# A transformer-like layer on one core: all chains of the activation sums ahead of the 1/rms scaling, in the openings of both SwiGLUs

## The chip, the core and the metric

The kernel runs on one core of a Trainium2 chip. The core has TensorE (PE: matmuls), VectorE (DVE) and ScalarE (ACT) for element by element work, GpSimd (POOL) and SyncE (SP), which issues the DMAs here. Each engine works through its own queue in order; semaphores make one wait for another. The metric is the device time of one execution in microseconds, the median of several runs.

## The reference

The layer has 1024 tokens of width 1024, in float32. What the change touches are the two SwiGLU sub-layers, the first and the last of four:

```python
def rmsnorm(x, g):
    y = xf * lax.rsqrt(jnp.mean(xf * xf, axis=-1, keepdims=True) + EPS)
    return (y * g.astype(jnp.float32)).astype(x.dtype)

def swiglu(h, w_gu, w_down):
    gate, up = jnp.split(h @ w_gu, 2, axis=-1)
    return (jax.nn.silu(gate) * up) @ w_down

x = x + 0.5 * swiglu(rmsnorm(x, ffn1_norm), ffn1_w_gu, ffn1_w_down)
...
x = x + 0.5 * swiglu(rmsnorm(x, ffn2_norm), ffn2_w_gu, ffn2_w_down)
```

The hidden width is 2816. Between the two stand two token mixers and a cross attention; they and the final norm are the same in both kernels.

## The kernel before, in words

Activations are held with the width on the 128 partitions and the tokens along the row: `x{c}_{hf}` is chunk `c` (0 to 7) of the width and half `hf` (0, 1) of the tokens, 128 x 512. A float32 product is made of three matmuls in the format fp32r: every operand is split into a high part (ACT copies it) and a low part (DVE subtracts), and high x high, high x low and low x high are added up in a PSUM bank. The gain is applied to x beforehand; the factor 1/rms belongs to a token and is multiplied in after the matmul (`rs`, a tile for each half of the tokens).

The SwiGLU's products go through a Strassen-Winograd scheme on 2 x 2 blocks: seven products instead of eight (`PRODUCTS`, line 235), from sums of the weights (`S1` to `S4`, made on POOL) and sums of the activations (`T1` to `T4`). The products of a job accumulate in three bank names X, Y, Z with two banks each. For a job the order is A11 into X, S1 x T1 into Y, S2 x T2 into X, A12 into Z, S3 x T3 into X, S4 into Y, A22 x T4 into X. After A11, S1 and S2 ACT copies the bank to SBUF (`e<-X`, `e<-Y`, `E<-X`); the next product into the bank waits for that copy.

The sums of the activations are made for four quarters `j` (two chunks of the width each) by `sums_12` (line 657), a generator that is one chain: POOL forms the difference `S<-x,x`; ACT makes the high part of T1 and a scaled copy `e` or `t`; DVE makes the low part of T1 and then T2 in `e` or `t`; ACT makes T2's high part and DVE its low part. A slot for `S` is one of three, so the fourth difference needs the first chain's slot back, when ACT and DVE have read it. `flow` (line 641) writes several chains in turns, a step of each. `sums_4` and `sums_3` make T4 and T3 later.

The opening of a SwiGLU, up to `pairs.run()` (line 968), runs ahead of the scheme. The first two columns of gate and up are computed plainly, eight chunks each (`plain`, and the gates before it): in the first SwiGLU the gates lie in PSUM banks X and Y, in the second (`stored`) they were computed earlier, written to DRAM and loaded again, half of them into a slot for weights (`r`). `scaled` (line 909) multiplies a gate column by `rs` on DVE and applies SiLU on ACT; the first SiLU needs a table load. `between` (line 929) is a generator that scales the four gate columns and then has `pairs.start` write the first loads, sums and splits of the scheme's weights. It is written as a third chain among `sums_12`, with a width of three chains.

In the first SwiGLU 1/rms comes from eight squares of token rows on ACT (line 470); the tiles of the last four are loaded once the first four are done with. A root of twelve small DVE steps follows, then PE spreads it over the partitions (line 218) and ACT copies it to `rs`. In the second SwiGLU the root is done before the opening.

The order of each engine is set by the written order: `in_order` (line 70) makes every instruction issued through `dve`, `act`, `pl_` and `pe` follow the one issued before on that engine, and all the steps above go through it. Instructions outside it (the squares, the root, the first factors) are fitted in between by the framework's scheduler when the kernel is built. In the profile most of these lines show as the helper's line 82.

Of the kernel before, what the change touches and what calls it, by code (L numbers as in the profile page):

```python
# [8 lines left out]
F32 = mybir.dt.float32  # L9
# [9 lines left out]
P = 128  # L19
# [3 lines left out]
H = 512  # L23
# [8 lines left out]
def hybrid_layer(ctx, tc, x, x_cols, mem, gains, ffn1_w_gu, ffn1_w_down, w_in, w_out, mem_w_q, mem_w_kv, mem_w_o,  # L32
# [6 lines left out]
    def pool(stack, name, bufs=1, space=None, side=None):  # L39
        kw = {} if space is None else {"space": space}  # L40
        if side:
            kw["side"] = side
        return stack.enter_context(tc.tile_pool(name=name, bufs=bufs, reuse_waits="tile", **kw))
# [386 lines left out]
    with ExitStack() as st:  # L430
# [48 lines left out]
        for e in range(2):  # L479
            own, other = (slice(64 * i, 64 * i + 64) for i in (e, 1 - e))  # L480
            t = maskp.tile([P, P], F32R, name=f"swap{e}")
# [4 lines left out]
        for n in (1, 2):  # L486
# [22 lines left out]
            for i in range(2):  # L509
                t = maskp.tile([P, P], F32R, name=f"yy{n}_{i}")  # L510
# [92 lines left out]
    def slot(blk, key, j):  # L603

        if key in ("T1", "T2", "T4"):
            t = blk.sum_slot(key, j)
            return t[:, 0, :], t[:, 1, :]
        c, hf = {"B11": (2 * j, 0), "B21": (2 * j + 1, 0), "B22": (2 * j + 1, 1), "T3": (2 * j, 1)}[key]
        return hp.tile([P, H], F32R, name=f"hh{c}_{hf}"), hp.tile([P, H], F32R, name=f"hl{c}_{hf}")
# [4 lines left out]
    def swiglu(rs, ys, g0, w_gu, w_down, blk, first, tag, done, tail, head, stored=False, hook=None, side=None, plain_last=False, lift=None):  # L614
        with ExitStack() as st:
# [19 lines left out]
            def quarter(j):  # L635
                return ([xT[2 * j + k, hf] for k in range(2) for hf in range(2)]
                        + [G[:, g0 + 2 * j + k:g0 + 2 * j + k + 1] for k in range(2)])
# [3 lines left out]
            def flow(chains, width):  # L641

                chains, active = list(chains), []
                while chains or active:
                    while chains and len(active) < width:
                        active.append(chains.pop(0))
                    active = [c for c in active if next(c, active) is not active]

            def chain_part(key, src, j):
                hi, lo = slot(blk, key, j)  # L650
                act.activation(hi, src, AF.Copy)
                yield
                dve.tensor_tensor(lo, src, hi.bitcast(F32), op=ALU.subtract)
                B[key].append((hi, lo))
                yield

            def sums_12(j, t):
                x11, x12, x21, x22, g1, g2 = quarter(j)
                d = blk.sp.tile([P, 4, P], F32, name="S").rearrange("p a b -> p (a b)")
                ts[j] = t  # L660
                hi, lo = slot(blk, "T1", j)
                pl_.tensor_tensor(d, x12, x11, op=ALU.subtract)
                yield
                act.activation(hi, d, AF.Copy, scale=g1)
                act.activation(t, d, AF.Copy, scale=g1)
                yield
                dve.scalar_tensor_tensor(lo, d, g1, hi.bitcast(F32), op0=ALU.mult, op1=ALU.subtract)
                B["T1"].append((hi, lo))
                dve.scalar_tensor_tensor(t, x22, g2, t, op0=ALU.mult, op1=ALU.subtract)
                yield  # L670
                yield from chain_part("T2", t, j)
# [10 lines left out]
            def sums_4(j):  # L682
                x11, x12, x21, x22, g1, g2 = quarter(j)
                dve.scalar_tensor_tensor(ts[j], x21, g2, ts[j], op0=ALU.mult, op1=ALU.subtract)
                yield
                yield from chain_part("T4", ts[j], j)
# [220 lines left out]
            pairs = weave(*streams)  # L907

            def scaled(out, src, hf):
                to = src if stored else out  # L910
                dve.tensor_tensor(to, src, rs[hf], op=ALU.mult)
                yield
                act.activation(out, to, AF.Silu)
                yield
# [13 lines left out]
            tp = pool(tps, "tp", 2)  # L928
            def between():
                for hf, src in ((0, early), (1, late)):  # L930
                    for m in range(2):
                        yield from scaled(s[hf][m], src[m], hf)
                pairs.start(1)
                yield
                pairs.start(2)
                yield
                pairs.start(3)

            flow([sums_12(j, pools["e0"].tile([P, H], F32, name="e") if j < 2 else tp.tile([P, H], F32, name="t"))
                  for j in range(2)] + [between()]  # L940
                 + [sums_12(j, tp.tile([P, H], F32, name="t")) for j in range(2, 4)], 3)
            flow([sums_4(0), sums_4(1)], 2)
            for m in range(2):
                dve.tensor_tensor(s[0][m], s[0][m], ups[0][m], op=ALU.mult)
# [47 lines left out]
    def to_mixers(acc, psn, psg, sgp):  # L992
        for c in range(DC):
# [4 lines left out]

    xs = {}
    swiglu(rs1, [y1[:, 0:4], y1[:, 4:8]], GF1, ffn1_w_gu, ffn1_w_down, blk1, first, "f", lambda d, hf, sqp, acc: arrive(d, hf, GMIX, sqp, acc, False, (d, hf) in ((7, 0), (6, 1))),  # L1000
           to_mixers, gps, hook=lower_bound, side=normalise_memory, lift=GMIX)
    f1.close()
# [664 lines left out]
    with ExitStack() as f2:  # L1667
        blk2 = blocks(f2, True)
        first = [blk2.load(ffn2_w_gu, 0, 4, FF)]
        swiglu(rs, ys2, GF2, ffn2_w_gu, ffn2_w_down, blk2, first, "g", arrive_last, finish, gd, True, plain_last=True)  # L1670
# [30 lines left out]
```

## Time and profile before

| | |
|---|---|
| median of 3 runs | 2307.11 us (2306.14 to 2309.64) |
| the profiled execution's time | 2306.37 us |
| its span, first to last instruction | 2304.7 us |
| PE busy | 2222.0 us, 96% |
| DVE, ACT, POOL busy | 73%, 43%, 32% |
| PE's mean granted clock | 0.988 |
| first opening in the trace | from 7 us to 72 us |
| second opening | from 1646 us to 1687 us |

Sums are made against the profiled execution, whose time is 0.74 us below the median. Matmuls overlap a little, so a row's duration is not the step from one to the next.

### The profile page before, as it was taken

How to read it: one execution, taken by the hardware profiler on the slowest of the kernel's cores; microseconds unless marked ns; L12 is line 12 of the kernel's file. 1: busy time of each engine (PE TensorE's matmuls, PEld its weight loads, DVE VectorE, ACT ScalarE, POOL GpSimd, SP SyncE). 2: the span in 40 equal slices, each digit the busy share in tenths (PEclk: the TensorE clock that was granted, in tenths of full speed). 3: DMA queues.
4: the chain of work that ended last, by engine and by line, in shares of the span. 5: the costliest groups of instructions: out<-in, count | busy, mean ns of one | idle time of the engine just before them, and what ended most of it. 6: DMA issues, size and time to landing. Idle time of an engine off the chain costs nothing. (4 is left out here: it accounts for less than half of the span.)

```text
span 2304.7 us, 31240 instructions
## 1 busy us (share of the span) xinstructions
PE 2222.0 (96%) x11240; PEld 1863.5 (81%) x11240; DVE 1681.3 (73%) x2816; ACT 984.1 (43%) x1877; POOL 732.8 (32%) x685
## 2 busy tenths in 40 slices
PE   8899999999999999999989999999989999999997
PEld 7788888778778797888879888887778888878876
DVE  6877778868976869778697546567587676885796
ACT  6544444443345526344364333224454343444324
POOL 3353536534541102010031020001335353653553
PEclk9999999999989999999999999999999999999999
DMA  8344443666721000100115311111334333366652
GB/s 293 115 137 136 139 136 134 241 217 216 238 94 38 28 20 28 32 24 28 38 30 163 110 37 56 46 37 42 124 110 138 112 135 119 128 239 215 194 174 74
DMA packets 220571, 265.80 MB, mean 115 GB/s; under 512 B 13440, under 2 KB 144512, under 8 KB 220416
## 3 DMA queue, kind: packets, MB, share of 16 engines
q1 hardware_dynamic: 220416, 263.80, 34.6%
q8 instruction: 89, 1.46, 0.3%
q14 instruction: 66, 0.54, 0.1%
HBM read 187.47 MB, written 76.28 MB: 114 GB/s over the span
## 5 line engine op out<-in xcount | busy, mean ns | idle before, releaser
L82 PE MATMUL X<-T,f 128*128 128x512 f32 x1464 | 348.4, 394 | 12.9 <-ACT e L82 12.6
L82 PEld LDWEIGHTS X<-T,f 128*128 128x128 f32 x1464 | 277.6, 190 | 72.5 <-ACT e L82 13.5
L82 PE MATMUL X<-hh,f 128*128 128x512 f32 x975 | 315.1, 394 | 8.8 <-DVE E L82 7.8
L82 ACT ACTIVATE f<-S 128x512 fp32r<-128x512 f32 (+2 forms) x256 | 155.3, 608 | 266.0 <-POOL S L82 252.3
L82 DVE TENSOR_TENSOR f<-S,f 128x512 fp32r<-128x512 f32 (+2 forms) x256 | 233.7, 925 | 38.8 <-ACT f L82 38.2
L82 PEld LDWEIGHTS X<-hh,f 128*128 128x128 f32 x975 | 184.6, 189 | 51.1 <-issue 9.2
L82 POOL TENSOR_TENSOR E<-E,rs 128x512 f32<-128x512 f32 x112 | 183.3, 1637 | 123.1 <-DVE E L82 102.7
L82 DVE TENSOR_TENSOR f<-r,f 128x512 fp32r<-128x512 f32 (+2 forms) x192 | 202.4, 1071 | 0.1
L82 PE MATMUL X<-hl,f 128*128 128x512 f32 x488 | 192.1, 394 | 2.9 <-DVE hl L82 2.9
L82 POOL TENSOR_TENSOR S<-r,r 128x512 f32<-128x512 f32 (+2 forms) x64 | 94.0, 1469 | 304.0 <-DMA r<-in_ffn_w_down_dram 84.8
L82 PE MATMUL Y<-T,f 128*128 128x512 f32 x732 | 176.4, 390 | 0.0
L82 PE MATMUL Z<-hh,f 128*128 128x512 f32 x488 | 161.0, 390 | 0.0
L82 PE MATMUL Y<-hh,f 128*128 128x512 f32 x488 | 160.9, 390 | 0.0
L82 PEld LDWEIGHTS Y<-T,f 128*128 128x128 f32 x732 | 137.5, 188 | 28.5
L127 PE MATMUL acc<-hh,wh 128*128 128x512 f32 (+1 forms) x384 | 153.7, 400 | 3.5 <-DVE E L82 3.2
L128 PE MATMUL acc<-hl,wh 128*128 128x512 f32 (+1 forms) x384 | 145.9, 380 | 1.9 <-DMA hl<-msl 1.9
L82 POOL TENSOR_TENSOR S<-S,r 128x512 f32<-128x512 f32 (+2 forms) x64 | 83.5, 1304 | 197.5 <-DVE f L82 173.3
L129 PE MATMUL acc<-hh,wl 128*128 128x512 f32 (+1 forms) x384 | 145.9, 380 | 0.0
L1123 POOL TENSOR_SCALAR_AFFINE_SELECT om<-om 128x128 f32<-128x128 f32 x64 | 26.8, 418 | 357.4 <-ACT om L1118 357.2
L82 DVE TENSOR_TENSOR E<-X,E 128x512 f32<-128x512 f32 x98 | 67.3, 687 | 93.1 <-PE X L82 92.4
L82 ACT ACTIVATE E<-X 128x512 f32<-128x512 f32 x102 | 60.4, 592 | 170.8 <-PE X L82 170.8
L107 ACT ACTIVATE wh<-wraw 128x512 fp32r<-128x512 f32 (+1 forms) x128 | 79.0, 654 | 106.4 <-PE acc L128 39.8
(453 smaller groups left out, 5476.5 us busy)
## 6 DMA issues: line engine op xcount, KB each, us to landing
r<-in_ffn_w_gu_dram SPq DMA_DIRECT2D x86, 512.0 KB, 3.6
r<-in_ffn_w_down_dram SPq DMA_DIRECT2D x32, 512.0 KB, 4.1
wraw<-in_w_in_dram SPq DMA_DIRECT2D x20, 512.0 KB, 3.6
wraw<-in_mem_w_kv_dram SPq DMA_DIRECT2D x16, 512.0 KB, 3.8
x<-in_x_cols_dram SPq DMA_DIRECT2D x16, 256.0 KB, 5.4
T<-in_x_dram SPq DMA_DIRECT2D x8, 512.0 KB, 6.4
fx<-x SPq DMA_DIRECT2D x16, 256.0 KB, 5.1
sg<-fx SPq DMA_DIRECT2D x16, 256.0 KB, 4.2
```

What stands on the lines that cost most here:

```text
L82: done = getattr(self.eng, name)(*args, **kw)
L107: nc.scalar.activation(hi[:, part], src[:, part], AF.Copy)
L127: nc.tensor.matmul(ps, lh, rh, start=start, stop=False)
L128: nc.tensor.matmul(ps, lh, rl, start=False, stop=False)
L129: last_mm[0] = nc.tensor.matmul(ps, ll, rh, start=False, stop=stop).ins
L1123: nc.gpsimd.affine_select(out=a[:, dg], in_=a[:, dg], compare_op=ALU.is_gt, fill=fill, base=0, pattern=[[-1, P]], channel_multiplier=1)
```

## The change

The four chains of `sums_12` are written in one `flow` of width three. `between`, which scales the gate columns, is written behind them. The first loads, sums and splits of the scheme (`pairs.start`) move into a function `factors_first`: in the first SwiGLU it is called at the end of `between` as before, in the second ahead of it. No instruction is added or removed, and no tile changes its size.

```diff
                 for hf, src in ((0, early), (1, late)):
                     for m in range(2):
                         yield from scaled(s[hf][m], src[m], hf)
-                pairs.start(1)
-                yield
-                pairs.start(2)
-                yield
-                pairs.start(3)
+                if not stored:
+                    factors_first()
+
+            def factors_first():
+                for n in (1, 2, 3):
+                    pairs.start(n)
 
             flow([sums_12(j, pools["e0"].tile([P, H], F32, name="e") if j < 2 else tp.tile([P, H], F32, name="t"))
-                  for j in range(2)] + [between()]
-                 + [sums_12(j, tp.tile([P, H], F32, name="t")) for j in range(2, 4)], 3)
+                  for j in range(4)], 3)
+            if stored:
+                factors_first()
+            for _ in between():
+                pass
             flow([sums_4(0), sums_4(1)], 2)
```

How it moves the instructions is shown at three places. Names carry the tile's number behind the underscore: `T12` is the sum T1 of quarter 2, `T20` the sum T2 of quarter 0.

ACT in the first opening, from the first factor of the up columns (line 422) on; the rows of line 470 are the squares. Before:

```order
L422 ACTIVATE f_542<-r0_141 128x512 [waits DMAHW3_49]
L422 ACTIVATE f_545<-r1_143 128x512 [waits DMAHW4_49]
L422 ACTIVATE f_548<-r0_141 128x512
L470 ACTIVATE T43_322,ss8_321<-T43_322 128x1024 [waits DMAHW5_49]
L470 ACTIVATE T40_325,ss8_321<-T40_325 128x1024 [waits DMAHW6_49]
L470 ACTIVATE T41_328,ss8_321<-T41_328 128x1024 [waits DMAHW7_49]
L470 ACTIVATE T42_331,ss8_321<-T42_331 128x1024 [waits DMAHW0_49]
L422 ACTIVATE f_551<-r1_143 128x512 [waits DVE_49,PE_49]
L470 ACTIVATE T43_334,ss8_321<-T43_334 128x1024 [waits DMAHW1_49,Activation_49]
```

And now:

```order
L422 ACTIVATE f_542<-r0_141 128x512 [waits DMAHW3_49]
L82 ACTIVATE T12_642<-S_641,G_83 128x512 [waits Pool_49]
L82 ACTIVATE t_633<-S_641,G_83 128x512
L422 ACTIVATE f_545<-r1_143 128x512 [waits DMAHW4_49]
L422 ACTIVATE f_548<-r0_141 128x512
L82 ACTIVATE T20_656<-e_631 128x512 [waits DVE_49]
L470 ACTIVATE T43_322,ss8_321<-T43_322 128x1024 [waits DMAHW5_49]
L82 ACTIVATE T21_658<-e_632 128x512 [waits DVE_49]
L470 ACTIVATE T40_325,ss8_321<-T40_325 128x1024 [waits DMAHW6_49]
L82 ACTIVATE T22_660<-t_633 128x512 [waits DVE_49]
L470 ACTIVATE T41_328,ss8_321<-T41_328 128x1024 [waits DMAHW7_49]
L82 ACTIVATE T13_666<-S_665,G_83 128x512 [waits Pool_49]
```

Six of the chains' copies stand between the factors and among the squares now (two more follow, behind the fifth and the sixth square), and five of these six rows wait for DVE or POOL.

DVE in the first opening. Before, behind the root (its last step is the row just ahead of these):

```order
L79 TENSOR_TENSOR sg_624<-X_145,rs0_584 128x512 [waits Activation_49]
L82 SCALAR_TENSOR_TENSOR T10_636<-S_635,G_83,T10_636 128x512 [waits Pool_49]
L82 SCALAR_TENSOR_TENSOR e_631<-x1_1_127,G_83,e_631 128x512
L82 SCALAR_TENSOR_TENSOR T11_639<-S_638,G_83,T11_639 128x512 [waits Pool_49]
L82 SCALAR_TENSOR_TENSOR e_632<-x3_1_131,G_83,e_632 128x512
L82 TENSOR_TENSOR sg_625<-Y_156,rs0_584 128x512
L82 TENSOR_TENSOR T20_652<-e_631,T20_652 128x512 [waits Activation_49]
L82 TENSOR_TENSOR T21_654<-e_632,T21_654 128x512 [waits Activation_49]
L82 TENSOR_TENSOR sg_626<-X_239,rs1_591 128x512 [waits PE_49]
```

Now, ahead of the root; the rows of line 191 and 423 are splits that stood there before as well:

```order
L82 SCALAR_TENSOR_TENSOR e_631<-x1_1_127,G_83,e_631 128x512
L191 SCALAR_TENSOR_TENSOR hl7_1_312<-x7_1_139,G_83,hh7_1_311 128x512 [waits DMAHW2_49,Activation_49]
L82 SCALAR_TENSOR_TENSOR T11_639<-S_638,G_83,T11_639 128x512 [waits Pool_49]
L423 TENSOR_TENSOR f_542<-r0_141,f_542 128x512 [waits DMAHW3_49,Activation_49]
L82 SCALAR_TENSOR_TENSOR e_632<-x3_1_131,G_83,e_632 128x512
L423 TENSOR_TENSOR f_545<-r1_143,f_545 128x512 [waits DMAHW4_49,Activation_49]
L423 TENSOR_TENSOR f_548<-r0_141,f_548 128x512 [waits Activation_49]
L82 SCALAR_TENSOR_TENSOR T12_642<-S_641,G_83,T12_642 128x512 [waits Pool_49]
L82 SCALAR_TENSOR_TENSOR t_633<-x5_1_135,G_83,t_633 128x512
L82 TENSOR_TENSOR T20_656<-e_631,T20_656 128x512 [waits Activation_49]
L82 TENSOR_TENSOR T21_658<-e_632,T21_658 128x512 [waits Activation_49]
L82 TENSOR_TENSOR T22_660<-t_633,T22_660 128x512 [waits Activation_49]
```

The chains stood behind the scaling `sg_624<-X_145,rs0_584`, which waits for ACT's copy of 1/rms; they stand ahead of the root now, and the scaling is the first row behind it.

DVE in the second opening, behind the low parts of the up factors. Before:

```order
L82 TENSOR_TENSOR sg_15882<-sg_15882,rs0_15842 128x512 [waits DMAHW2_49,Activation_49,Pool_49]
L82 SCALAR_TENSOR_TENSOR T10_15899<-S_15898,G_83,T10_15899 128x512 [waits Pool_49]
L82 SCALAR_TENSOR_TENSOR e_15894<-x1_1_11857,G_83,e_15894 128x512
L82 SCALAR_TENSOR_TENSOR T11_15902<-S_15901,G_83,T11_15902 128x512 [waits Pool_49]
L82 SCALAR_TENSOR_TENSOR e_15895<-x3_1_12803,G_83,e_15895 128x512
L82 TENSOR_TENSOR sg_15883<-sg_15883,rs0_15842 128x512 [waits DMAHW3_49]
L82 TENSOR_TENSOR T20_15915<-e_15894,T20_15915 128x512 [waits PE_49,Activation_49]
L82 TENSOR_TENSOR T21_15917<-e_15895,T21_15917 128x512 [waits PE_49,Activation_49]
L82 TENSOR_TENSOR r0_15886<-r0_15886,rs1_15849 128x512 [waits DMAHW7_49]
L82 TENSOR_TENSOR r0_15886<-r0_15886,rs1_15849 128x512 [waits DMAHW4_49]
```

And now:

```order
L82 SCALAR_TENSOR_TENSOR T10_15899<-S_15898,G_83,T10_15899 128x512 [waits Activation_49]
L82 SCALAR_TENSOR_TENSOR e_15894<-x1_1_11857,G_83,e_15894 128x512 [waits Activation_49]
L82 SCALAR_TENSOR_TENSOR T11_15902<-S_15901,G_83,T11_15902 128x512 [waits Activation_49]
L82 SCALAR_TENSOR_TENSOR e_15895<-x3_1_12803,G_83,e_15895 128x512 [waits Activation_49]
L82 SCALAR_TENSOR_TENSOR T12_15905<-S_15904,G_83,T12_15905 128x512 [waits PE_49,Activation_49]
L82 SCALAR_TENSOR_TENSOR t_15896<-x5_1_11845,G_83,t_15896 128x512 [waits Activation_49]
L82 TENSOR_TENSOR T20_15919<-e_15894,T20_15919 128x512 [waits PE_49,Activation_49]
L82 TENSOR_TENSOR T21_15921<-e_15895,T21_15921 128x512 [waits PE_49,Activation_49]
L82 TENSOR_TENSOR T22_15923<-t_15896,T22_15923 128x512 [waits Activation_49]
L82 SCALAR_TENSOR_TENSOR T13_15929<-S_15928,G_83,T13_15929 128x512 [waits Activation_49]
L82 SCALAR_TENSOR_TENSOR t_15897<-x7_1_12747,G_83,t_15897 128x512 [waits Activation_49]
L82 TENSOR_TENSOR T23_15935<-t_15897,T23_15935 128x512 [waits Activation_49]
```

The scaling was first and the low parts of T12 and T13 came behind the first factor of the scheme; now all chains are done first, three low parts of the scheme's factors (`f`) follow, and the scaling is next.

## The prediction

> **What bounds the kernel now.** I began with the page's busy line and its group of TensorE's costliest waits, then the list of who waited for whom.
>
> ```profile
> PE 2222.0 (96%) x11240; PEld 1863.5 (81%) x11240; DVE 1681.3 (73%) x2816; ACT 984.1 (43%) x1877; POOL 732.8 (32%) x685
> PE X L82 <- ACT e L82: 12.6, 2, 6.7
> ```
>
> TensorE (PE) is busy 96% of the span, so an edit can earn only where PE stands still. The second row is PE's largest sum of waits: two waits on ScalarE's (ACT's) copy `e`, 12.6 us in all, one in each SwiGLU. The timeline of PE shows both.
>
> ```profile
> 57.20 2.88 PE L82 MATMUL Y<-T,f 128*128 128x512 f32 x12
> 66.75 5.49 PE L82 MATMUL X<-T,f 128*128 128x512 f32 x12 [6.67 <-ACT e L82]
> 72.03 0.53 PE L82 MATMUL Z<-hh,f 128*128 128x512 f32 x1
> ...
> 1673.49 2.88 PE L82 MATMUL Y<-T,f 128*128 128x512 f32 x12
> 1682.35 5.08 PE L82 MATMUL X<-T,f 128*128 128x512 f32 x12 [5.98 <-ACT e L82]
> 1687.28 0.40 PE L82 MATMUL Z<-hh,f 128*128 128x512 f32 x1
> ```
>
> In each opening the second sum product (T2 into bank X) starts 6.0 to 6.7 us late (a row: start, duration, engine, line, operation, tiles; in brackets the idle time before it and what ended it), and then takes 5.1 to 5.5 us, where the twelve matmuls of T1 just before took 2.88. The table by stretches gives the reason (columns: stretch; its length; busy time and count of PE, weight load, VectorE (DVE), ACT, POOL; granted clock; DMA share; GB/s):
>
> ```profile
> 62.00:72.20 10.20, 5.46 (x13) 4.30 (x14) 9.67 (x17) 6.23 (x12) 0.00 (x0) 0.50 0.13 51
> 1679.90:1686.70 6.80, 4.35 (x10) 3.49 (x11) 6.77 (x12) 3.70 (x8) 0.00 (x0) 0.51 0.21 80
> ```
>
> After the idle stretch the granted clock is half. So a stall is paid twice. From the end of T1 to the first Z matmul the first opening takes 72.03 − 60.08 = 11.95 us, the second 1687.28 − 1676.37 = 10.91; twelve matmuls at full clock advance the queue by 2.72 (the quoted 2.88 less the overlap of the last one). **Recoverable: 9.2 us and 8.2 us.**
>
> Why is ACT late? Its queue and DVE's, first opening:
>
> ```profile
> 62.84 1.29 ACT L82 ACTIVATE T<-e 128x512 fp32r<-128x512 f32 x2 [3.75 <-DVE e L82]
> 66.12 0.57 ACT L82 ACTIVATE e<-X 128x512 f32<-128x512 f32 x1
> 39.81 0.69 DVE L79 TENSOR_TENSOR sg<-X,rs 128x512 f32<-128x512 f32 x1 [2.68 <-ACT rs L221]
> 59.73 2.35 DVE L82 TENSOR_TENSOR T<-t,T 128x512 fp32r<-128x512 f32 x2
> 41.29 1.68 POOL L82 TENSOR_TENSOR S<-x,x 128x512 f32<-128x512 f32 x1 [22.72 <-DMA fx<-x]
> 1654.80 0.69 DVE L82 TENSOR_TENSOR sg<-sg,rs 128x512 f32<-128x512 f32 x1 [5.35 <-ACT rs L221]
> 1656.29 1.68 POOL L82 TENSOR_TENSOR S<-x,x 128x512 f32<-128x512 f32 x1 [14.04 <-DVE T L82]
> 1656.73 1.79 DVE L82 SCALAR_TENSOR_TENSOR T<-S,G,T 128x512 fp32r<-128x512 f32 x1
> ```
>
> `e<-X` stands behind T4's first parts on ACT, these behind DVE's `e`, that behind the low parts of T2 (59.73). And all DVE work of the chains stands behind one instruction, the scaling `sg<-X,rs`, which needs 1/rms. While it waits, POOL idles 22.72 and 14.04 us, because the fourth difference needs a slot that DVE must first free (the first row names the DMA; the order of instructions has POOL wait for DVE). The last row shows a DVE step that takes 1.79 us while POOL works.
>
> **The change, second opening.** The 16 chain steps of DVE now stand ahead of the scaling, and ACT's chain steps stand around the two copies of rs. 1/rms itself isn't touched: its root stands ahead of all this on DVE, and PE's spread of it releases ACT as before:
>
> ```profile
> 1646.95 2.50 DVE L423 TENSOR_TENSOR f<-r,f 128x512 fp32r<-128x512 f32 x4 [2.88 <-ACT f L422]
> 1654.11 0.60 ACT L221 ACTIVATE rs<-nm 128x512 f32<-128x512 f32 x1 [3.18 <-PE nm L218]
> ```
>
> I walk the queues from the rows: from start to start DVE takes 0.66 us a step, ACT 0.61 with a gain and 0.53 without (rows of the first opening, below), POOL 1.7, and DVE stands still while POOL works. DVE is free at 1649.4 (first row's end). POOL's fourth difference (to 1651.9) and first weight sum (to 1654.3) hold DVE up twice; the chains end at 1660.1, the first factors and S2 at 1665.2, the scaling at 1667.7, the SiLUs on ACT at 1669.4. PE needs none of these before 1676.4: its plain columns read the factors and bank X is not held by the stored gates. The ACT copies T2 of chains 0 and 1 end at 1653.7, ahead of the rs copy at 1654.11.
>
> What comes later are the SiLUs, and with them a load of weights:
>
> ```profile
> 1662.72 1.24 ACT L82 ACTIVATE sg<-r 128x512 f32<-128x512 f32 x2 [1.17 <-DVE r L82]
> DMA to landing us min/median/max: 3.3/3.3/3.3
> 1686.56 0.58 ACT L82 ACTIVATE e<-Y 128x512 f32<-128x512 f32 x1
> 1692.72 0.58 ACT L82 ACTIVATE E<-X 128x512 f32<-128x512 f32 x1
> ```
>
> Before, the SiLUs end at 1663.96 (first row). They free a slot for weights, whose next load leaves then and lands 3.3 us later (second row). With the change it leaves at 1669.4 and lands at 1672.7; POOL's sum for the next job ends at 1674.5, ACT's factor at 1675.1, `e<-X` at 1675.8. PE wants it at 1676.4, so the wait is gone with 0.6 us to spare. Next late is T3: from `e<-Y` to `E<-X` ACT takes 6.2 us; starting at 1678.4, it frees bank X at 1685.2, where PE comes at 1684.5: 0.7 us, against 0.4 in the run before. Gain 8.2 − 0.4 = **7.8 us**, bounds 5.0 (load and T3 each 1.5 later than walked) and 8.2.
>
> **The change, first opening.** Here 1/rms isn't ready early: its eight squares run on ACT during the same time, and the chains move in among them.
>
> ```profile
> 21.36 0.70 ACT L82 ACTIVATE e<-S,G 128x512 f32<-128x512 f32 x1
> 21.97 1.66 ACT L422 ACTIVATE f<-r 128x512 fp32r<-128x512 f32 x3
> 23.53 1.04 ACT L470 ACTIVATE T<-T 128x1024 f32<-128x1024 f32 x1
> 29.00 0.63 ACT L422 ACTIVATE f<-r 128x512 fp32r<-128x512 f32 x1 [1.21 <-PE X L129]
> 34.51 0.18 ACT L470 ACTIVATION_READ_ACCUMULATOR T<-T 128x1 f32 x1
> 20.51 2.72 DVE L191 SCALAR_TENSOR_TENSOR hl<-x,G,hh 128x512 fp32r<-128x512 f32 x4
> 34.73 0.17 DVE L158 TENSOR_SCALAR ms<-ss 128x8 f32<-128x8 f32 x1 [4.37 <-ACT T L470]
> 36.96 0.17 DVE L164 SCALAR_TENSOR_TENSOR y8h<-u,y8h 128x8 f32<-128x8 f32 x1
> 38.09 1.05 PE L218 MATMUL nm<-ident,y8h 128*128 128x128 f32 x8
> DMA to landing us min/median/max: 5.7/5.7/5.7
> ```
>
> Today the squares end at 34.69, the root at 37.13, and PE comes to the spread of 1/rms at 38.09: a reserve of under 1 us. Now: T1's low part of chain 0 stands first on DVE and POOL's fourth difference then holds DVE to 20.9. DVE's rows follow at 0.66: `e` of chain 0 done 24.8, of chain 1 27.4, `t` of chain 2 29.95. ACT, at 24.8 after two more chain steps, must wait for each in turn: T2 of chain 0 to 25.4, square 1 to 26.5, T2 of chain 1 not before 27.5, square 2 at 29.1, T2 of chain 2 not before 30.05, square 3 at 31.65, T1 of chain 3, square 4 at 33.3, the fourth up factor 33.85, square 5, `t`, square 6 at 36.55, T2 of chain 3, squares 7 and 8: 39.3. (Each of the last four loads leaves when its tile's first square is done; the last leaves at 33.4 and, by 5.7 us as in the last row, lands at 39.1: then 40.2. The first of them, sent alone, took 3.5; the spacing is wider now, so I take 39.3.) The root takes 2.4 more: 41.8. POOL's first weight sum will now run about then; in the other opening it cost the root about this:
>
> ```profile
> 1638.04 4.22 POOL L82 TENSOR_TENSOR S<-x,x 128x512 f32<-128x512 f32 x3
> 1641.07 1.22 DVE L160 TENSOR_SCALAR y4h<-b 128x4 int32<-128x4 int32 x1
> ```
>
> One step of 0.17 became 1.22. I take 0.8 for it: 42.6. **New PE stall: 42.6 − 38.1 = 4.5 us**, bounds 3.8 (no collision) and 5.8 (late load, full collision).
>
> What it does to the clock, from two other stalls of this kernel and what followed:
>
> ```profile
> 443.28 0.47 PE L82 MATMUL X<-hh,f 128*128 128x512 f32 x1 [4.17 <-DVE E L82]
> 444.30:447.60 3.30, 3.30 (x10) 2.56 (x9) 3.27 (x4) 0.63 (x1) 3.30 (x3) 0.51 1.06 407
> 1296.95 0.33 PE L1026 MATMUL tr<-ident,yy 128*128 128x128 f32 x1 [2.21 <-DVE yy L1022]
> 1297.60:1301.00 3.40, 3.40 (x10) 2.57 (x9) 1.10 (x2) 0.63 (x1) 0.00 (x0) 0.52 0.40 112
> ```
>
> 4.17 us of idling led to 3.4 us at half clock, so 1.7 us lost; bounds 0.9 (half of it falls into the idle time) and 3.4 (twice that). [...]
>
> PE then runs through: T1 ends at 60.08 + 4.5 + 1.7 = 66.3. `e<-X` is ready about 64.2, since ACT has nothing of T2 left before it. So the stall of 6.67 and its half clock go. Bank X of the plain columns is freed by the scaling at about 44, wanted at 49. Gain 9.2 − 4.5 − 1.7 = **3.0 us**, bounds 9.2 − 5.8 − 3.4 = 0.0 and 9.2 − 3.8 − 0.9 = 4.5.
>
> The rest costs nothing: no instruction is added or removed; SP keeps its order, and the x tiles that it writes out leave some 5 us later, and their room is wanted first by `E<-X`, behind T3. Behind the openings the order of every engine is the same, and PE bound, so what is gained stays.
>
> **Sum:** 7.8 + 3.0 = 10.8 us. Against the profiled execution, 2306.4 us with a span of 2304.7, that is 2295.6; the median of the three runs lies 0.7 higher, so **2296.3 us**.
>
> **Rivals.**
> 1. *Both gains nearly whole.* DVE's first steps come sooner than walked, the squares slip by 2 us rather than 4.6, the spread waits 1 us: 9 − 1 + 8.2, about 16 us, 2291. For it: ACT's added work ahead of square 8 is only 4.6 us (four steps of 0.61, four of 0.53), and 1.2 us of it fits in today's gap (the row at 29.00). Against it: ACT must wait for DVE three times.
> 2. *One opening gives nothing.* The last square load at 5.7 us and full collision in the first opening (0.0), and the weight slot's load coming 2 us later than walked in the second, so that PE waits again (8.2 − 4 = 4): 2303, within what counts as no change. For it: the reserve of only 0.6 us. Against: its queue is short, and the load had the DMA to itself before (3.3).
> 3. *Slower.* Place: DVE ahead of the root in the first opening. If POOL held DVE for every chain step (1.79 rather than 0.66, as at 1656.73), the squares would come 1.1 us later for each of some ten steps, the root at 54, the PE stall 16 us: 9.2 − 16 − 1.7 + 7.8 = −0.7. It is slower by more than 0.2% only from a root later than 58 us. Against it: POOL has a single instruction to run there before the weights land.
> 4. *The order isn't what the words say.* It is: ACT, DVE and POOL rows show all four chains ahead of the scaling in both places.
>
> **How the numbers follow.** Forecast 0.65, rival 1 0.16, rival 2 0.14, rival 3 0.05. A measurement here tells 0.2%, 4.6 us. The forecast's own range is 2294.4 to 2302.1 (bounds above: 4.5 + 8.2 = 12.7 to 0.0 + 5.0 us of gain). Low end towards rival 1: 2291; high end with rival 2: 2303. Faster by over 0.2% (below 2302.5): the forecast, rival 1 and some of rival 2: 0.85; the same 0.11; slower 0.04.
>
> **What would show it.** Right: no PE wait on `e` in either opening; T2's twelve matmuls near 2.9 us; a new wait of PE of 4 to 5 us at the spread, with the root's first step at about 39.3 instead of 34.73; a half-clock stretch after it; POOL's fourth difference at 19 us. Wrong: the first step of the root before 37 (then rival 1); PE still waiting for `e` at 1676; or a new wait in T3.

## The result, and the profile after

The changed kernel takes **2296.64 us** (median of 4 runs, 2294.18 to 2297.65), the kernel before beside it 2308.38 us (2306.14 to 2310.47). The ratio is 0.9948, with a 95% interval of 0.9931 to 0.9965: 11.7 us faster. The forecast was 10.8 us and 2296.3 us.

TensorE's busy line and its wait at the spread of 1/rms, from the page and from the list of waits of the changed kernel:

```profile
PE 2220.7 (97%) x11240; PEld 1864.1 (81%) x11240; DVE 1681.7 (73%) x2816; ACT 983.8 (43%) x1877; POOL 730.9 (32%) x685
PE nm L218 <- DVE y8h L164: 5.0, 1, 5.0
```

The wait on `e` (12.6 us in two) is no longer in that list, and there is one of 5.0 us that the kernel before didn't have. To measure each opening by itself I take the time from the first Z matmul of its plain columns to the first Z matmul behind the product of T2. Of the kernel before the prediction shows the ends (72.03 and 1687.28); these are the starts, and its wait in T3:

```profile
30.84 0.39 PE L127 MATMUL Z<-hh,f 128*128 128x512 f32 x1
...
1646.97 0.50 PE L127 MATMUL Z<-hh,f 128*128 128x512 f32 x1 [1.20 <-ACT f L422]
...
1693.35 0.50 PE L82 MATMUL X<-hh,f 128*128 128x512 f32 x1 [0.43 <-ACT E L82]
```

The timeline of PE in the changed kernel:

```profile
31.46 0.39 PE L127 MATMUL Z<-hh,f 128*128 128x512 f32 x1
...
43.83 2.05 PE L218 MATMUL nm<-ident,y8h 128*128 128x128 f32 x8 [4.96 <-DVE y8h L164]
...
68.53 2.88 PE L82 MATMUL X<-T,f 128*128 128x512 f32 x12
71.25 0.39 PE L82 MATMUL Z<-hh,f 128*128 128x512 f32 x1
...
1648.21 0.50 PE L127 MATMUL Z<-hh,f 128*128 128x512 f32 x1 [1.20 <-ACT f L422]
...
1677.45 2.88 PE L82 MATMUL X<-T,f 128*128 128x512 f32 x12
1680.17 0.39 PE L82 MATMUL Z<-hh,f 128*128 128x512 f32 x1
```

T2's twelve matmuls now take 2.88 us in both places, with no idle time ahead of them. The first opening went from 72.03 − 30.84 = 41.19 us to 71.25 − 31.46 = 39.79, a gain of **1.40**. The second went from 1687.28 − 1646.97 = 40.31 to 31.96, a gain of **8.35**, and the wait of 0.43 us in T3 is gone too. So the openings give 10.2 us. The span is shorter by 2304.7 − 2295.4 = 9.3 us. Between the openings, 71.25 to 1648.21, the changed kernel took 1576.96 us, the one before 1574.94: 2.0 us longer in work that the change does not touch. The head of the kernel was 0.6 us longer as well, and what lies behind the second opening, T3's wait apart, 1.8 us shorter: 10.2 − 2.0 − 0.6 + 1.8 is the 9.3, with roundings. The granted clock shows a difference between the openings, at 1224, that the kernel before did not have; PE's wait for a load just ahead of it, at 1222.46, was 3.30 us, where the kernel before waited 1.89 (columns as in the prediction; the first row is the first opening, the last is spoken of further down):

```profile
43.00:49.90 6.90, 6.07 (x22) 5.57 (x23) 1.91 (x5) 3.08 (x5) 0.26 (x1) 0.51 1.05 403
1224.00:1230.90 6.90, 6.90 (x36) 6.90 (x34) 2.56 (x8) 1.09 (x2) 0.00 (x0) 0.51 0.38 125
2048.30:2051.70 3.40, 3.36 (x15) 2.82 (x16) 3.37 (x4) 1.53 (x3) 2.83 (x2) 1.00 1.05 404
```

### The profile page after: what moved, and what is told of

It is laid out like the page before. It is cut to its first block, busy times and chain, and to the rows that moved or that the text cites. A ratio compares the mean times of both kernels' runs of the same rounds, so it can differ in the third digit from the quotient of the medians.

```text
span 2295.4 us, 31243 instructions
## 1 busy us (share of the span) xinstructions
PE 2220.7 (97%) x11240; PEld 1864.1 (81%) x11240; DVE 1681.7 (73%) x2816; ACT 983.8 (43%) x1877; POOL 730.9 (32%) x685
## 4 chain that ended last, share of the span: by engine, by line
PE 80%; DVE 11%; ACT 3%; issue 3%; DMA 2%; POOL 1%; SPq 0%; POOLq 0%; DVEq 0%; ACTq 0%
PE X L82 26%; PE Y L82 13%; PE Z L82 6%; PE acc L127 5%; PE acc L129 4%; PE acc L128 4%; PE q L128 2%; PE q L127 2%; PE q L129 2%; DVE om L1130 2%; PE z L1307 2%; DVE E L82 1%; PE wo L129 1%; PE wo L127 1%; PE wo L128 1%
## 5 line engine op out<-in xcount | busy, mean ns | idle before, releaser
L82 PE MATMUL X<-T,f 128*128 128x512 f32 x1464 | 343.5, 389 | 0.3 <-DVE T L82 0.2
```

What stands on the lines that cost most here:

```text
L82: done = getattr(self.eng, name)(*args, **kw)
```

## The experiments

A time is to be read against that of the kernel before on the same chip; the stage lengths are from one profiled execution of each kernel, and tell more, since they leave out what happens elsewhere. The intervals of root_first, two_chains, keep_busy and factors_behind all overlap with that of the changed kernel, so what sets these four apart from it is read from the stages and the traces, not from the times.

| kernel | us, median (range) | before beside it | ratio, 95% | first opening | second opening |
|---|---|---|---|---|---|
| before | | | | 41.19 | 40.31 |
| changed | 2296.64 (2294.2–2297.7) | 2308.38 | 0.9948 (0.9931–0.9965) | 39.79 | 31.96 |
| second_only | 2298.74 (2295.5–2304.1) | 2310.06 | 0.9957 (0.9943–0.9972) | 41.21 | 31.95 |
| first_only | 2306.83 (2299.9–2312.8) | 2310.06 | 0.9986 (0.9974–0.9999) | 39.09 | 39.84 |
| root_first | 2294.63 (2289.6–2299.0) | 2310.06 | 0.9940 (0.9927–0.9954) | 35.70 | 31.95 |
| changed_again | 2297.83 (2295.8–2298.5) | 2310.06 | 0.9952 (0.9940–0.9964) | 39.80 | 31.95 |
| two_chains | 2290.73 (2286.9–2296.0) | 2308.35 | 0.9926 (0.9910–0.9941) | 32.77 | 31.95 |
| keep_busy | 2294.29 (2290.6–2299.9) | 2308.35 | 0.9941 (0.9926–0.9956) | 36.88 | 31.96 |
| factors_behind | 2300.07 (2295.5–2306.0) | 2308.35 | 0.9964 (0.9952–0.9977) | 39.61 | 32.13 |

**One opening at a time.** The change stands under a condition, `stored` in second_only (shown) and `not stored` in first_only; otherwise the order of the kernel before is kept (`first_sums` are the four chains), and `between` starts the first factors as it did there:

```diff
             if stored:
...
+                flow(first_sums, 3)
...
+                for _ in between():
+                    pass
+            else:
+                flow(first_sums[:2] + [between()] + first_sums[2:], 3)
```

> The change in the second opening alone; the first opening is as before. Theory (the traces of before and after read by stretches): the second opening gives some 8.4 us of the gain, the first 1.4. So 2308.4 - 8.4 = 2300 us; TensorE's two waits on ScalarE's e become one, 6.7 us at 66.8; the second sum product follows the first without a gap near 1680. Rival: the first opening gives as much as its upper bound, 4.5 us, and the rest of the 11.7 us comes from the second: then 2301.5 to 2303 us.

> The change in the first opening alone; the second is as before. Theory: a gain of 1.4 us, 2307 us: the wait of 6.7 us on e and its half clock (9.2 us together) go, a wait of 5.0 us at the spread of 1/rms and two windows of half clock come. The wait of 6.0 us near 1682 stays. Rival: the first opening is worth 4.5 us, so 2304 us.

The second product of each opening in the PE timeline, second_only first:

```profile
67.03 5.49 PE L82 MATMUL X<-T,f 128*128 128x512 f32 x12 [6.70 <-ACT e L82]
...
1680.72 2.88 PE L82 MATMUL X<-T,f 128*128 128x512 f32 x12
```

and first_only, with the spread:

```profile
43.34 2.05 PE L218 MATMUL nm<-ident,y8h 128*128 128x128 f32 x8 [5.16 <-DVE y8h L164]
...
1682.42 4.61 PE L82 MATMUL X<-T,f 128*128 128x512 f32 x12 [6.00 <-ACT e L82]
```

Each half shows its own waits, and the other opening keeps its length to 0.5 us (41.21 against 41.19, 39.84 against 40.31). The half clock that first_only expects shows in the matmuls behind its wait: from 45.6 to 46.9 they stand 0.42 to 0.43 us apart, as in the changed kernel's stretch at 0.51, and from 48.3 on 0.23. Most of the gain is the second opening's: 11.3 us of time in second_only (8.4 in the stage), 3.2 us in first_only (2.1 in the stage). The rival, 4.5 us from the first opening, isn't in the stages; the times alone, whose intervals reach from 0.2 to 6 us for first_only, could not have told.

**What made 1/rms late.** In root_first, ScalarE's copies of T2 are issued behind the eighth square, and VectorE's low parts of T2 behind the root's last step; since both engines keep the order of the chains, all that follows them in the chains stands behind too:

```diff
+                squared = nc.scalar.activation(tok, tok, AF.Square, ...).ins
...
+            rooted[0] = eng.scalar_tensor_tensor(y, u, 1.5, y, ...).ins
...
-                act.activation(hi, src, AF.Copy)
...
+                if key == "T2" and not stored:
+                    with tc.issue_after(squared):
+                        act.activation(hi, src, AF.Copy)
...
+                    with tc.issue_after(rooted[0]):
+                        dve.tensor_tensor(lo, src, hi.bitcast(F32), op=ALU.subtract)
```

> As the changed kernel, but in the first opening ScalarE's copies of T2 (and all of the chains that follows them) are issued behind the eighth square, and VectorE's low parts of T2 behind the last step of the root. Theory: what made 1/rms late is that ScalarE waited for VectorE's chain steps among the squares. Now the squares end near 35, the root near 37.4, TensorE doesn't wait at the spread (5.0 us before) and keeps its clock (3 us lost before); T2 still is ready before TensorE asks for it, so no wait on e. Gain over the changed kernel 8 us: 2289 us. Rival 1: the squares' loads set the time, so the squares still end at 39 or later and nothing changes: 2296.6. Rival 2: the chains, now behind the root, come too late for T1 or T2, and a wait on e returns: 2296 or more.

The spread on PE, a square on ACT, a step of the root on DVE and POOL's first sum of weights, from its timelines:

```profile
40.37 1.58 PE L220 MATMUL nm<-ident,y8h 128*128 128x128 f32 x8 [2.03 <-DVE y8h L166]
...
34.28 1.06 ACT L472 ACTIVATE T<-T 128x1024 f32<-128x1024 f32 x1 [0.64 <-DMA T<-in_x_dram]
...
38.34 1.28 DVE L166 SCALAR_TENSOR_TENSOR y8h<-u,y8h 128x8 f32<-128x8 f32 x1
...
38.33 1.26 POOL L82 TENSOR_TENSOR S<-r,r 128x512 f32<-128x512 f32 x1 [16.94 <-DVE u L165]
```

The cause is as the theory says, and its size is not: the squares ended at 36.7, where they ended at 40.3 in the changed kernel, the wait fell from 5.0 to 2.0 us and the opening from 39.8 to 35.7, 4.1 us and not 8. The clock was not kept either: behind the wait the matmuls stand 0.42 to 0.43 us apart from 42.2 to 43.5, as in the changed kernel's stretch at 0.51, and 0.23 us from 45.0 on. It cost 1.7 us: with the wait of 2.03 us taken off, the opening is that much above the 31.96 us that it takes with neither (worked out below). The squares ended at 36.7 rather than 35. Two steps of the third chain still stood ahead of the first square, so the last four loads, each of which leaves when an earlier square is done, left later; and the root was then caught by POOL's weight sum (1.28 us for a step of 0.17). Neither rival holds: the squares ended before 39, though their loads held up two of them, by 1.23 and 0.64 us, and no wait on `e` came back.

That the root meets POOL's sum does not look like chance. The sum starts 1.63 us behind the root's first step in the changed kernel (41.98 and 40.35) and 1.61 us behind it here (38.33 and 36.72), though the root stands 3.6 us earlier. SP issues the sum's load right behind the last load of the squares, in the changed kernel at 33.89, 0.45 us after the fourth square's end at 33.44; here that square ends at 29.49, so the load can leave earlier by as much. Both profiles name a step of the root as what the sum waits for; so the tie through the load is argued, not shown.

So two_chains opens two chains at a time in the first opening:

```diff
-                  for j in range(4)], 3)
+                  for j in range(4)], 3 if stored else 2)
```

> As root_first, and in the first opening only two chains are open at a time instead of three, so that ScalarE does no step of the third chain ahead of the squares. Theory: in root_first the squares ended 2 us late because two steps of the third chain (1.2 us) stood ahead of them, and their last loads left that much later; the root then ran into GpSimd's weight sum. Now the squares end near 35 as in the kernel before, the root near 37.4, ahead of GpSimd's sum; TensorE doesn't wait at the spread and keeps its clock; from T1 to the first Z matmul of the next product there is no gap either. Against the changed kernel the first opening is 8 us shorter: about 2289 to 2290 us. Rival: six to eight chain steps of VectorE now stand between the root and the scaling, so bank X isn't free when TensorE wants it at 43.8: a wait of 1 to 3 us there, with half clock behind it, and 2292 to 2296 us.

Its PE timeline, with a step of the root and POOL's sum:

```profile
39.35 1.13 PE L220 MATMUL nm<-ident,y8h 128*128 128x128 f32 x8 [0.42 <-DVE y8h L166]
...
61.57 2.88 PE L82 MATMUL X<-T,f 128*128 128x512 f32 x12
64.29 0.39 PE L82 MATMUL Z<-hh,f 128*128 128x512 f32 x1
...
70.57 0.50 PE L82 MATMUL X<-hh,f 128*128 128x512 f32 x1 [0.68 <-ACT E L82]
...
37.38 1.22 DVE L166 SCALAR_TENSOR_TENSOR y8h<-u,y8h 128x8 f32<-128x8 f32 x1
...
37.29 1.29 POOL L82 TENSOR_TENSOR S<-r,r 128x512 f32<-128x512 f32 x1 [16.23 <-DVE u L164]
```

The opening is 32.77 us, 8.4 less than before and 7.0 less than in the changed kernel; 0.68 us of it is given back in T3, where PE now comes earlier than `E<-X`. The wait for bank X that the rival foresaw is not there. Its time is **2290.73 us, ratio 0.9926 (0.9910 to 0.9941)**: faster than the kernel before by 13.6 to 20.8 us, and in this stage faster than the changed kernel. One part of the theory failed: the root is not ahead of POOL's sum, which came earlier with it (37.29, 1.53 us behind the root's first step at 35.76). One step took 1.22 us instead of 0.17, and these 1.05 us are more than the 0.42 us that PE still waits.

**What the half clock costs.** keep_busy lets PE run 22 matmuls of no use ahead of the spread, where it would idle:

```diff
+            def busy():
+                filler = psn.tile([P, H], F32, name="nm")
+                for _ in range(22):
+                    with tc.issue_after(last_mm[0]):
+                        last_mm[0] = nc.tensor.matmul(filler, up[0, 0][0][:, 0, :], hT[0][0][0], ...).ins
+                spread_both(rs, ys, psn, "nm", last_mm[0])
...
+            ups[0].append(plain(up, 1, 0, u_banks[1], None if stored else busy))
```

> The changed kernel with 22 matmuls more in the first opening, just ahead of the spread, whose result nobody uses (the spread overwrites it). They take 22 x 0.227 = 5.0 us, as long as TensorE waits there. Theory: the wait itself can't be won back this way, but half clock after it comes from TensorE's idling alone, so the stretch of 6.8 us at half clock goes, and with it 3.0 us: the first Z matmul behind T2 at about 68.3 instead of 71.25; some 2294 us. Rival: half clock there has another cause (the start of the kernel, the transfers that run at the same time); then the stretch stays and the time is the changed kernel's.

The filler on PE's timeline, and the clock in two stretches (the second is spoken of below):

```profile
39.31 5.15 PE L707 MATMUL nm<-hh,f 128*128 128x512 f32 x22
44.56 1.13 PE L218 MATMUL nm<-ident,y8h 128*128 128x128 f32 x8
```

```profile
38.00:50.00 12.00, 12.00 (x62) 9.94 (x61) 5.71 (x17) 5.69 (x10) 1.29 (x1) 1.00 1.03 374
1290.00:1297.00 7.00, 7.00 (x31) 5.62 (x32) 2.67 (x4) 1.27 (x2) 0.00 (x0) 1.00 0.43 111
```

The clock is whole from 38 to 50, although the transfers of that stretch ran as before (DMA share 1.03, and 1.05 from 43 to 49.9 in the changed kernel). The opening is 36.88 us against 39.79: the half clock had cost **2.9 us** in that profile, and in this one, where PE doesn't idle there, there is none.

**The same kernel twice.**

> The changed kernel once more, unaltered, beside the three others. [...] Time 2296.6 within 2 us. [...] Rival: half clock follows from the program alone; then the same stretches stand in the same places.

A wait of PE far from the openings, in the first profile of the changed kernel (the clock behind it is the last row of the table above):

```profile
2048.34 0.47 PE L82 MATMUL X<-hh,f 128*128 128x512 f32 x1 [3.10 <-DVE E L82]
```

and in the second, with its wait at the spread and the clock behind the far wait:

```profile
43.81 2.04 PE L218 MATMUL nm<-ident,y8h 128*128 128x128 f32 x8 [5.57 <-DVE y8h L164]
...
2043.93 0.47 PE L82 MATMUL X<-hh,f 128*128 128x512 f32 x1 [3.10 <-DVE E L82]
```

```profile
2045.20:2048.60 3.40, 3.40 (x10) 2.68 (x9) 3.40 (x3) 1.06 (x2) 3.40 (x3) 0.52 1.05 404
```

One kernel, one wait of 3.10 us: whole clock behind it in the first profile, 3.4 us of half clock in the second. Near 1220 the second profile has 3.4 us of half clock, the first 6.9. The time came within 1.2 us of that expected. The stages of the openings came out alike to 0.01 us, for the first opening by luck: PE waited 5.57 us at the spread, 4.96 in the first profile, and half clock cost 2.3 and 2.9 us behind it. (The opening takes 41.19 − 9.23 = 31.96 us with neither; what exceeds it and the wait is put down to the clock.) So half clock does not follow from the program alone, and the rival falls. It doesn't follow the length of the wait either: in keep_busy, PE's 2.20 us of idling ahead of 1289.97 left the clock whole (the table above), where 2.21 us at the same place halved it in the kernel before (the prediction shows it at 1296.95).

```profile
1289.97 0.33 PE L1040 MATMUL tr<-ident,yy 128*128 128x128 f32 x1 [2.20 <-DVE yy L1036]
```

**Where the first factors stand.** factors_behind puts them behind the scaling in the second opening, as they are in the first:

```diff
-                if not stored:
-                    factors_first()
+                factors_first()
...
-            if stored:
-                factors_first()
```

> The changed kernel, but in the second opening the first weight factors stand behind the scaling, as in the first opening. It tests one part of the change by itself: where the factors stand. Theory: the gain of the second opening comes from the chains ahead of the scaling; VectorE has time for factors and scaling in either order, so no wait comes back, 2296.6 us within the measurement. Rival: the factors' place is needed too: S1's or S2's factor then comes late and TensorE waits 1 to 4 us at T1 or T2, with half clock behind it: 2298 to 2302 us.

The spread of the first opening, T2 and the first wait in T3 of the second on its PE timeline:

```profile
44.39 2.05 PE L218 MATMUL nm<-ident,y8h 128*128 128x128 f32 x8 [5.87 <-DVE y8h L164]
...
1681.96 3.01 PE L82 MATMUL X<-T,f 128*128 128x512 f32 x12
...
1692.95 0.50 PE L82 MATMUL X<-hh,f 128*128 128x512 f32 x1 [2.53 <-ACT E L82]
```

The theory was wrong. T2 came just in time, 0.2 us being lost in the stage, but T3 came 2.5 us late and 3.4 us of half clock followed; the time is 2300.07 us, 8.3 under the kernel before beside it, not 12. It is the wait in the trace that decides here; the interval of the time (5.3 to 11.1 us under) does not exclude the changed kernel. The rival had the right sign at the wrong place. The chains ahead of the scaling end the wait on `e`; the factors ahead of it keep the next wait from growing.

## Why the prediction was right, step by step

**Second opening (7.8 us forecast, 8.35 measured, and 0.43 more in T3).** The walk of the queues, from the timelines of the changed kernel (subtract 1648.21 − 1646.97 = 1.24 us to compare with the times forecast):

```profile
1660.56 0.69 DVE L82 TENSOR_TENSOR T<-t,T 128x512 fp32r<-128x512 f32 x1 [0.70 <-ACT T L82]
...
1664.74 1.11 DVE L82 TENSOR_TENSOR f<-S,f 128x512 fp32r<-128x512 f32 x1 [1.84 <-ACT f L82]
...
1666.97 1.28 DVE L82 TENSOR_TENSOR r<-r,rs 128x512 f32<-128x512 f32 x2
...
1668.88 1.13 ACT L82 ACTIVATE sg<-r 128x512 f32<-128x512 f32 x2
...
1668.96 1.78 POOL L82 TENSOR_TENSOR S<-r,r 128x512 f32<-128x512 f32 x1 [3.67 <-DMA r<-in_ffn_w_gu_dram]
1670.69 1.76 POOL L82 TENSOR_TENSOR S<-r,S 128x512 f32<-128x512 f32 x1
...
1674.92 0.60 ACT L82 ACTIVATE e<-X 128x512 f32<-128x512 f32 x1 [1.78 <-PE X L82]
```

The chains end at 1661.25 − 1.24 = 1660.0 (1660.1 forecast), S2's factor at 1664.6 (1665.2), the scaling at 1667.0 (1667.7), the SiLUs at 1668.8 (1669.4). One step was wrong, on the safe side: that POOL's sum hangs on the load that the SiLUs release. POOL's wait for weights ended at 1668.96, before the SiLUs were done: SP had issued that load at 1665.32, when POOL's sum before it was done, and only the next one, at 1670.04, waited for the SiLUs. (In the kernel before it was the load of 1663.99 that waited for the SiLUs.) POOL's sums ended at 1672.45 − 1.24 = 1671.2, not 1674.5, and `e<-X` waited for nothing but PE's own product. It had 1677.45 − 1675.52 = 1.9 us to spare, not 0.6. With that T3 came earlier too: no wait, where I had 0.7 us. So all of the recoverable time came back.

**First opening (3.0 us forecast, 1.40 measured, bounds 0.0 to 4.5).** The mechanism was right to the instruction. ACT waits for DVE among the squares, then for the last load; DVE runs the root; POOL runs beside it:

```profile
27.59 0.63 ACT L82 ACTIVATE T<-e 128x512 fp32r<-128x512 f32 x1 [0.92 <-DVE e L82]
...
30.12 0.63 ACT L82 ACTIVATE T<-t 128x512 fp32r<-128x512 f32 x1 [0.85 <-DVE t L82]
...
39.17 1.06 ACT L470 ACTIVATE T<-T 128x1024 f32<-128x1024 f32 x1 [0.95 <-DMA T<-in_x_dram]
...
40.35 0.17 DVE L158 TENSOR_SCALAR ms<-ss 128x8 f32<-128x8 f32 x1 [2.44 <-ACT T L470]
...
42.17 1.12 DVE L162 TENSOR_TENSOR u<-y8h 128x8 f32<-128x8 f32 x1
...
41.98 1.28 POOL L82 TENSOR_TENSOR S<-r,r 128x512 f32<-128x512 f32 x1 [21.01 <-DVE u L163]
```

The root's first step is at 40.35; the walk gave 39.3, or 40.2 with a last load at 39.1, and it was the load (0.95 us of waiting at 39.17). POOL's sum made one root step 1.12 us instead of 0.17, 0.95 us where I took 0.8. So the root ended at 43.69, 1.1 us later than the 42.6 of the walk. PE's wait is 4.96 us (4.5 forecast, bounds 3.8 to 5.8), closer than that, because PE itself came to the spread late, at 38.87 instead of 38.09; 0.6 us of this it has from the head of the kernel, where ACT and DVE are not late. In the three other profiles with this first opening the wait was 5.16 (first_only), 5.57 (changed_again) and 5.87 us (factors_behind).

The term that was mis-sized is **the clock behind that wait: 1.7 us taken, 3.0 measured**. From 43.0 to 49.9 the clock was 0.51; PE idled for the first 0.83 us of it, so (6.9 − 0.83) × 0.49 = 3.0 us were lost, and keep_busy gave 2.9 back. I had taken one stretch of 3.4 us from the wait of 4.17 us at 443; here it was twice that, and 6.8 us again in factors_behind, from 41.3 to 48.1, 3.1 us of it in the wait. In changed_again, first_only and factors_behind what exceeds the wait and the 31.96 us is 2.3, 2.0 and 1.8 us. What the opening pays is the sum of wait and clock, and that was 7.1 to 7.8 us in the four profiles, where the forecast had 4.5 + 1.7 = 6.2. With both sizes put right, 9.2 − 4.96 − 3.0 = 1.2, close to the 1.40.

**The sum** came out right because these misses offset each other: the first opening gave 1.6 us less than forecast, the second with T3 1.0 more, so 10.2 instead of 10.8. That the offsets nearly cancel, and that 2296.3 and 2296.64 agree to 0.3 us, is luck; the mechanism is not. The remaining 1.5 us up to the 11.7 of the medians is inside their interval (8 to 16 us).

**The rivals.** Both gains nearly whole: no, the squares slipped by 5 us, not 2; two_chains shows what that would have been worth. One opening giving nothing: nearly so for the first, 1.4 us, but the second lost none. Slower, by POOL holding DVE at every step: no; POOL had one sum to run there, as the forecast said. The order is as the words say.

## What to carry to other kernels

Work moved into an engine's idle time is only free if what stands behind it in that queue is not wanted sooner: here the chains filled VectorE's wait for 1/rms, and in one place they delayed 1/rms itself, through ScalarE's squares and the loads that these release. Before such a move, list what each touched queue still owes to the thing the wait was for, put that ahead by an explicit order, and move only the rest (two_chains: an opening 7 us shorter than with the plain move). Look also at what is tied to the work that you move: here POOL's sum started 1.53 to 1.63 us behind the root's first step in three different orders. And price a wait of TensorE with the clock behind it, as a range: in these profiles it cost from 0 us (behind 3.10 us of idling near 2045) to 3.4 us (behind 3.30 us at 1222, 6.9 us at 0.51).

## What the runs showed of the hardware

In the five profiles read through in steps of 1 us (before, changed, two_chains, keep_busy, factors_behind) the stretches at half clock are 3.4, 6.8, 10.2 or 13.6 to 13.7 us long, the last one aside, which ends with the span. Whether a wait is followed by one can differ between executions of the same kernel: 3.10 us of idling near 2045 cost nothing in one profile of the changed kernel and 3.4 us at half clock in the next. What decides it no run shows. Added up over the whole span, these five executions spent between 35.7 us (keep_busy) and 63.4 us (factors_behind) at half clock; half of that difference, 14 us, is more than the change is worth. These two executions took 2290.6 and 2306.0 us. The scatter of the times goes with the clock also where the kernel is the same: of the 17 executions of the kernel before that stand beside root_first, the three with the lowest mean clock, 0.985, took 2313.4 to 2315.5 us, the seven with 0.988 to 0.990 took 2305.8 to 2308.5 us.

A step of the root (128 x 8) takes 0.17 us by itself. Where it met POOL's sum of 128 x 512 it took 1.12 us (changed), 1.28 (root_first) and 1.22 (two_chains), one step in each. A chain step of DVE (128 x 512) that takes 0.75 us by itself took 1.79 and 1.76 us at 1651.93 and 1654.31 in the changed kernel, beside POOL's instructions of 1.67 and 1.59 us. So the walk's "DVE stands still while POOL works" fits these places, but not all: in the kernel before, `sg<-Y,rs` at 44.11 took 0.68 us while POOL worked from 43.66 to 45.35.
